# A hybrid decoder trunk on one Trainium2 core: token tiles 2 to 7 of the first layer scaled from a feature-major copy of x in groups of 256 and 512 columns, the residual loaded from that copy

## The chip, the cores and the metric

The kernel runs on one core of a Trainium2 chip. The metric is the device time of one execution in microseconds (us). Five engines work side by side, each through its own instructions in order: PE (matrix products and transposes), DVE (VectorE), ACT (ScalarE), POOL (GpSimd) and SP, which issues most of the DMA transfers. They wait for each other through semaphores.

## The reference

The reference is a two-layer trunk over a residual stream x of 1024 tokens by 1024 features in f32. Each layer is, cut to what matters here:

```python
h = rmsnorm(x, norm1[l])          # x * rsqrt(mean(x*x) + 1e-6) * gain, per token
proj = h @ w_in[l]                # q, k, v of two attentions, and gates
o_a = dilated_mixture(...)        # windowed attention, three dilations
o_b = stick_breaking_attention(...)
merged = g_a * (o_a @ w_br_a) + g_b * (o_b @ w_br_b)
x = x + merged @ w_o[l]
h2 = rmsnorm(x, norm2[l])
x = x + conv_gated_ffn(h2)
```

and a last rmsnorm. What the change touches is the first rmsnorm of the first layer, which turns the input x into h, and the place that the first residual addition reads x from.

## The kernel before, in words

**Layout.** Products contract over features, so h is held feature-major: 128 features on the partitions, eight such blocks (k = 0 to 7), tokens along the free dimension. The 1024 tokens are two halves n = 0, 1 of 512, each of four token tiles of 128. Every f32 operand of a product is held as two fp32r parts, `hh` (rounded by ACT, L146) and `hl` (the rest, by DVE, L154; the helper is `split`), and a product is three matmuls for each k (L188 to L190).

**The start (`first`, from L2021).** It gets h from x tile by tile. SP loads token tile i token-major as `xr` (L2033, 512 KB, four buffers). ACT squares it with a sum over the row (L2063), takes the root (L2066), and DVE the reciprocal (L2067): the token's factor, a column `ss`. Tiles 0 and 1 are scaled token-major on DVE (L2074), turned by PE (`x_t<-xsq`, L2054) and split. For tiles 2 to 7, PE turns the raw tile (`x_t<-xr`, eight transposes of 128x128 for a tile, L2054), ACT copies it out of PSUM (`x_part`, L2083), PE spreads the factor over the partitions by one more transpose (`x_rb`, L2097), DVE multiplies block by block (`h_raw`, L2100, 128x128), and `split` makes `hh` and `hl`. Raw tiles 0 and 1 are turned and copied as well. Each pair of copies is stored to DRAM as `xs` (L2087, 1 MB each, four of them); the residual is loaded from there much later (`x_in`, L471). POOL puts the scaled tiles 0 and 1 together again as `h_raw` (L2120, `again`).

**What reads h first (`head`).** In order: the values of four heads for token tiles 0 to 3 (`v_ps`, 24 matmuls of 128x256 per tile), one pair of key and query products for half 0 (`kq_ps`, then `q_ps`, 24 matmuls of 128x512 each), the values of tiles 4 to 7, the same two products for half 1. `v_ps`, `kq_ps` and `q_ps` take turns in the two PSUM banks of the tag "ps": the values of tiles 4 and 5 use the bank of `kq_ps`, which is free once ACT and DVE have taken `kq_h` and `kq_l` out of it (L605, L606). The weights of the keys and queries (`kq_w`, two chunks each) are loaded by SP (L169, two buffers) and split on POOL (L176, L177). From then on the program is a long run of block products (`i_a`, `i_c` and others) with attention and FFN behind them.

**What sets the order.** PE's order is written out by hand: `mixer` steps the generator `first` and the generator `head` in turn. On ACT, DVE, POOL and SP the order is fixed when the program is built, by priorities; at run time each engine takes its instructions strictly in that order, and an instruction that waits holds all that are behind it.

## Time and profile before

| what | us |
|---|---|
| median of 3 runs | 2603.27 |
| lowest and highest | 2602.32, 2603.33 |
| the profiled execution, its own time | 2603.86 |
| its span, first to last instruction | 2602.2 |
| first `kq_ps` matmul of half 0 starts | 29.19 |
| first `v_ps` matmul of tile 4 starts | 42.23 |
| first `i_a` matmul starts | 65.46 |

The page gives the busy time of each engine, the chain of work that ended last, and the costliest groups of instructions. A row of a group reads: line, engine, operation, output and inputs, shape and count, then busy time, mean ns of one, and the idle time ahead of it with what ended it. A row of the timeline reads: start, length, engine, line, operation, and in brackets the idle time before. Matmuls are pipelined, so a row of eight is shorter than eight times the mean of one. The time of the profiled execution is 1.7 us more than its span.

### The profile page before, as it was taken

How to read it: one execution, taken by the hardware profiler on the slowest of the kernel's cores; microseconds unless marked ns; L12 is line 12 of the kernel's file. 1: busy time of each engine (PE TensorE's matmuls, PEld its weight loads, DVE VectorE, ACT ScalarE, POOL GpSimd, SP SyncE). 2: the span in 40 equal slices, each digit the busy share in tenths (PEclk: the TensorE clock that was granted, in tenths of full speed). 3: DMA queues.
4: the chain of work that ended last, by engine and by line, in shares of the span. 5: the costliest groups of instructions: out<-in, count | busy, mean ns of one | idle time of the engine just before them, and what ended most of it. 6: DMA issues, size and time to landing. Idle time of an engine off the chain costs nothing.

```text
span 2602.2 us, 36060 instructions
## 1 busy us (share of the span) xinstructions
PE 2589.6 (100%) x12647; PEld 2165.4 (83%) x12647; DVE 2084.7 (80%) x3485; ACT 1349.5 (52%) x2521; POOL 105.6 (4%) x145
## 2 busy tenths in 40 slices
PE   9999999999999999999999999999999999999999
PEld 8888888888888888888888888888888888888887
DVE  8877777796888888897677788777869888889965
ACT  6555666664554545422445555666645555554225
POOL 3000000030000000000000000000300000000000
PEclk9999999999999999999999999999999999999999
DMA  7434578863244454688344436798633354447863
GB/s 257 152 119 134 163 207 226 236 235 101 88 148 157 138 176 134 243 325 311 146 147 146 128 127 194 194 235 238 198 99 121 122 171 136 154 162 264 342 242 118
DMA packets 401409, 470.60 MB, mean 181 GB/s; under 512 B 24500, under 2 KB 315980, under 8 KB 399436
## 3 DMA queue, kind: packets, MB, share of 16 engines
q1 hardware_dynamic: 400364, 465.90, 55.2%
q0 software_dynamic: 704, 2.13, 0.4%
q8 instruction: 100, 1.64, 0.3%
q14 instruction: 81, 0.66, 0.1%
q10 hardware_dynamic: 160, 0.27, 0.0%
HBM read 305.59 MB, written 162.63 MB: 180 GB/s over the span
## 4 chain that ended last, share of the span: by engine, by line
PE 93%; DVE 3%; ACT 2%; DMA 1%; issue 1%; SPq 0%; POOL 0%; DVEq 0%; ACTq 0%
PE u_a L1060 6%; PE u_a L1061 6%; PE u_a L1059 6%; PE d_ps L1823 5%; PE d_ps L1825 5%; PE d_ps L1824 5%; PE i_a L1059 5%; PE i_a L1060 5%; PE i_a L1061 5%; PE u_c L1059 3%; PE u_c L1060 3%; PE u_c L1061 3%; PE i_c L1059 2%; PE i_c L1061 2%; PE i_c L1060 2%; PE o_ps L188 2%
## 5 line engine op out<-in xcount | busy, mean ns | idle before, releaser
L146 ACT CAST w_hi<-up_a 128x512 fp32r<-128x512 f32 x280 | 174.0, 622 | 277.1 <-DVE up_a L1677 120.8
L154 DVE TENSOR_TENSOR w_lo<-up_a,w_hi 128x512 fp32r<-128x512 f32 x280 | 189.3, 688 | 83.6 <-ACT w_hi L146 83.6
L146 ACT CAST w_hi<-in_a 128x512 fp32r<-128x512 f32 x252 | 156.2, 622 | 161.8 <-PE i_c L1060 35.6
L154 DVE TENSOR_TENSOR w_lo<-in_a,w_hi 128x512 fp32r<-128x512 f32 x252 | 172.7, 687 | 73.3 <-ACT w_hi L146 64.7
L1834 DVE TENSOR_TENSOR x<-x,d_ps 128x512 f32<-128x512 f32 x220 | 149.9, 683 | 60.3 <-PE d_ps L1825 57.0
L1059 PE MATMUL u_a<-hh,w_hi 128*128 128x512 f32 x320 | 124.5, 389 | 0.0
L1060 PE MATMUL u_a<-hl,w_hi 128*128 128x512 f32 x320 | 124.5, 389 | 0.0
L1061 PE MATMUL u_a<-hh,w_lo 128*128 128x512 f32 x320 | 124.5, 389 | 0.0
L1059 PE MATMUL u_a<-t_hi,w_hi 128*128 128x512 f32 x320 | 124.5, 389 | 0.0
L1060 PE MATMUL u_a<-t_lo,w_hi 128*128 128x512 f32 x320 | 124.5, 389 | 0.0
L1061 PE MATMUL u_a<-t_hi,w_lo 128*128 128x512 f32 x320 | 124.5, 389 | 0.0
L1823 PE MATMUL d_ps<-gd_in,w_hi 128*128 128x512 f32 x316 | 123.2, 390 | 0.0
L1825 PE MATMUL d_ps<-gd_in,w_lo 128*128 128x512 f32 x316 | 123.0, 389 | 0.0
L1824 PE MATMUL d_ps<-gd_in,w_hi 128*128 128x512 f32 x316 | 122.9, 389 | 0.0
L1059 PE MATMUL i_a<-hh,w_hi 128*128 128x512 f32 x288 | 117.9, 410 | 0.0
L1059 PE MATMUL i_a<-t_hi,w_hi 128*128 128x512 f32 x288 | 116.5, 404 | 0.0
L1061 PE MATMUL i_a<-hh,w_lo 128*128 128x512 f32 x288 | 113.1, 393 | 0.0
L1061 PE MATMUL i_a<-t_hi,w_lo 128*128 128x512 f32 x288 | 113.1, 393 | 0.0
L1060 PE MATMUL i_a<-hl,w_hi 128*128 128x512 f32 x288 | 112.9, 392 | 0.0
L1060 PE MATMUL i_a<-t_lo,w_hi 128*128 128x512 f32 x288 | 112.9, 392 | 0.0
L1823 PE MATMUL d_ps<-gd_in,wd 128*128 128x512 f32 x284 | 111.0, 391 | 0.0
L1825 PE MATMUL d_ps<-gd_in,wd 128*128 128x512 f32 x284 | 110.5, 389 | 0.0
(405 smaller groups left out, 7738.7 us busy)
## 6 DMA issues: line engine op xcount, KB each, us to landing
gd<-g SPq DMA_DIRECT2D x154, 512.0 KB, 3.1
gd_in<-gd SPq DMA_DIRECT2D x154, 512.0 KB, 6.2
up_a<-in_w_up_dram SPq DMA_DIRECT2D x80, 512.0 KB, 5.5
in_a<-in_w_in_dram SPq DMA_DIRECT2D x72, 512.0 KB, 5.4
wd_raw<-in_w_down_dram SPq DMA_DIRECT2D x22, 1024.0 KB, 11.4
gin<-gs SPq DMA_DIRECT2D x32, 512.0 KB, 4.3
w_raw<-in_w_o_dram SPq DMA_DIRECT2D x64, 256.0 KB, 2.8
gs<-u SPq DMA_DIRECT2D x48, 256.0 KB, 2.5
```

Of the source, the lines that this page charges most:

```text
L146: one = act.copy(hi, src)
L154: two = dve.tensor_tensor(lo, src, f32(hi), ALU.subtract)
L188: pe.matmul(o, lh, rh, start=(first and i == 0), stop=False, skip_group_check=share)
L1059: pe.matmul(o, w[0][:, c], rh, start=(first and i == 0), stop=False, skip_group_check=True)
L1060: pe.matmul(o, w[0][:, c], rl, start=False, stop=False, skip_group_check=True)
L1061: pe.matmul(o, w[1][:, c], rh, start=False, stop=(last and i == 3), skip_group_check=True)
L1823: pe.matmul(o, wh[:, c], gh, start=(i == 0 and k in (0, 4, 5)), stop=False, skip_group_check=True)
L1824: pe.matmul(o, wh[:, c], gl, start=False, stop=False, skip_group_check=True)
L1825: pe.matmul(o, wl[:, c], gh, start=False, stop=(i == m - 1), skip_group_check=True)
L1834: dve.tensor_tensor(x, x, o, ALU.add)
```

## The change

The program gets a second input, `xt`, which is x turned to feature-major, [128, 8, 1024]; it is laid out with the inputs, ahead of the launch.

Tiles 2 and 3: one load `x_late` of 128x8x256 from `xt`; two factor transposes; eight DVE multiplications of 128x256 instead of sixteen of 128x128; the splits in four pairs of k (128x2x256). Tiles 4 to 7: the half is loaded from `xt` straight into `h_raw` in two transfers of 128x4x512; four factor transposes in one place; eight DVE multiplications of 128x512 in place; eight splits of 128x512. The 64 transposes of raw tiles, the 16 copies out of PSUM and the four stores to `xs` are gone; the token-major tiles `xr` are still loaded, for the squares. The residual of layer 0 is loaded from `xt`.

```diff
-    def x_in(n, h):
+    def x_in(l, n, h):
...
+        src = xs[n][:, 4 * h : 4 * h + 4, :] if l else xt[:, 4 * h : 4 * h + 4, n * HF : (n + 1) * HF]
+        nc.sync.dma_start(X[n][h], src)
...
         def scaled(i):
...
-            ss = factor[i] = sb.tile([P, 8], F32, tag="ss", bufs=2, name="ss")
+            ss = factor[i] = sb.tile([P, 8], F32, tag="ss", bufs=2, name="ss") if i < 4 else wide[:, 2 * (i - 4) :]
             with tc.high_priority(offset=AHEAD):
                 one = act.activation(sq, xr[i], AF.Square, accum_out=ss[:, 0:1])
-                if i >= TWICE + 2:
-                    tc.add_manual_dep(one.ins, LAST["kept" if i == 5 else f"hi{max(2, i - 3)}"], NO_SYNC, reason="behind")
+                if i > 3:
+                    tc.add_manual_dep(one.ins, LAST["hi2"], NO_SYNC, reason="behind")
...
-        def normed(i):
+        def normed(i, many, src):
 
             n, c = i // 4, i % 4
-            if c == 0:
-                new_h(n)
-            if i in (TWICE, 4):
-                raw_h(n)
-            rb = bank("s" if i == TWICE else "o", "x_rb")
-            pe.transpose(rb[:, 0:P], factor[i][:, 2:3].to_broadcast([P, P]), ident)
-            t = slice(c * P, (c + 1) * P)
+            w = many * P
+            rb = bank("s" if n == 0 else "o", "x_rb")
+            for j in range(many):
+                pe.transpose(rb[:, j * P : (j + 1) * P], factor[i + j].to_broadcast([P, P]), ident)
+            t = slice(c * P, c * P + w)
             for k in range(KD):
-                dve.scalar_tensor_tensor(RAW[n, k // 4][:, k % 4, t], part[i][:, k, :], g0[:, k : k + 1], rb[:, 0:P], ALU.mult, ALU.mult)
...
+                h_ = RAW[n, k // 4][:, k % 4, t]
+                dve.scalar_tensor_tensor(h_, src(k), g0[:, k : k + 1], rb[:, 0:w], ALU.mult, ALU.mult)
+                if n or k % 2:
+                    kk = slice(k, k + 1) if n else slice(k - 1, k + 1)
+                    LAST["h"] = split(*(y[:, kk, t] for y in H[n]), RAW[n, k // 4][:, slice(kk.start % 4, kk.start % 4 + kk.stop - kk.start), t]).ins.name
+                    LAST.setdefault(f"hi{i}", LAST["hi"])
...
+        load(3)
+        late = quarter("x_late").rearrange("p a (b c) -> p (a b) c", c=2 * P)
+        nc.sync.dma_start(late, xt[:, :, 2 * P : 4 * P])
+        for i in (4, 5):
+            load(i)
+        raw_h(1)
+        for h in range(2):
+            nc.sync.dma_start(RAW[1, h], xt[:, 4 * h : 4 * h + 4, HF:T])
+        tps[1] = turned(rest[1], "s")
...
+        raw_h(0)
+        with tc.high_priority(offset=AHEAD):
+            normed(2, 2, lambda k: late[:, k, :])
+        yield
+        load(6)
+        load(7)
...
+        new_h(1)
+        normed(4, 4, lambda k: RAW[1, k // 4][:, k % 4, :])
...
+    inputs = {**inputs, "xt": np.asarray(inputs["x"])[0].T.reshape(KD, P, T).transpose(1, 0, 2)}
```

How the order of the instructions moves, at the three places that matter below. A row is a line of the kernel, the operation, what it writes and reads, and the shape; x2 is two alike in a row. Line numbers of the changed kernel are some lines off those of before.

ACT from the square of tile 3 on, before (`hh_194` is the half of tokens 0 to 511):

```order
L2063 ACTIVATE xsq,ss<-xr 128x1024
L2066 ACTIVATE ss<-ss,eps 128x1
L146 CAST hh_194<-h_raw 128x4x128 x2
L2063 ACTIVATE xsq,ss<-xr 128x1024
L585 CAST vb<-v_ps 128x4x2x64
L2066 ACTIVATE ss<-ss,eps 128x1
L2083 COPY x_part<-x_t 128x4x128 x2
L2063 ACTIVATE xsq,ss<-xr 128x1024
L146 CAST hh_194<-h_raw 128x4x128
L2066 ACTIVATE ss<-ss,eps 128x1
L2083 COPY x_part<-x_t 128x4x128 x2
L146 CAST hh_194<-h_raw 128x4x128
```

and in the changed kernel, from the same square on (`hh_195` is the same half; `wide` holds the factors of tiles 4 to 7):

```order
L2065 ACTIVATE xsq,ss<-xr 128x1024
L2068 ACTIVATE ss<-ss,eps 128x1
L146 CAST hh_195<-x_t 128x4x128 x2
L146 CAST hh_195<-h_raw 128x2x256
L2065 ACTIVATE xsq,wide<-xr 128x1024 x2
L146 CAST hh_195<-h_raw 128x2x256
L2068 ACTIVATE wide<-wide,eps 128x1 x2
L2065 ACTIVATE xsq,wide<-xr 128x1024
L146 CAST hh_195<-h_raw 128x2x256
L2068 ACTIVATE wide<-wide,eps 128x1
L2065 ACTIVATE xsq,wide<-xr 128x1024
L146 CAST hh_195<-h_raw 128x2x256
```

Before, both casts of tile 2 stand ahead of the square of tile 4, and the two of tile 3 behind the squares of tiles 4 and 5. Now there are four casts for tiles 2 and 3 together: the first stands ahead of the squares of tiles 4 and 5, the second behind them, the third behind the square of tile 6 and the fourth behind that of tile 7.

SP's transfers from the loads of `xr` 2 and 3 on, before:

```order
L2033 DMA xr<-in_x_dram 128x1024 x2
L169 DMA w_raw<-in_w_in_dram 128x4x128 x2
L2033 DMA xr<-in_x_dram 128x1024 x2
L2087 DMA xs_86<-x_part 1024x1x256
L169 DMA w_raw<-in_w_in_dram 128x4x128 x2
L2033 DMA xr<-in_x_dram 128x1024
```

and now:

```order
L2035 DMA xr<-in_x_dram 128x1024 x2
L2154 DMA x_late<-in_xt_dram 128x8x256
L2035 DMA xr<-in_x_dram 128x1024
L2159 DMA h_raw<-in_xt_dram 128x4x512
L2035 DMA xr<-in_x_dram 128x1024
L2159 DMA h_raw<-in_xt_dram 128x4x512
L2035 DMA xr<-in_x_dram 128x1024 x2
L169 DMA w_raw<-in_w_in_dram 128x4x128 x2
```

The three transfers from `xt` stand between the tiles, and the key weights (L169) have gone from behind tile 3 to behind tile 7.

DVE around `kq_l`, which frees the PSUM bank that the values of tile 4 need, before (`hl_444` is the half of tokens 512 to 1023):

```order
L2100 SCALAR_TENSOR_TENSOR h_raw<-x_part,g_85,x_rb 128x128 x6
L154 TENSOR_TENSOR hl_444<-h_raw,hh_443 128x4x128
L606 TENSOR_TENSOR kq_l<-kq_ps,kq_h 128x512
L154 TENSOR_TENSOR hl_444<-h_raw,hh_443 128x4x128
L2100 SCALAR_TENSOR_TENSOR h_raw<-x_part,g_85,x_rb 128x128 x8
```

and now (`hl_438` is the same half):

```order
L2091 SCALAR_TENSOR_TENSOR h_raw<-h_raw,g_85,x_rb 128x512 x3
L154 TENSOR_TENSOR hl_438<-h_raw,hh_437 128x512 x3
L2091 SCALAR_TENSOR_TENSOR h_raw<-h_raw,g_85,x_rb 128x512 x3
L154 TENSOR_TENSOR hl_438<-h_raw,hh_437 128x512 x3
L2091 SCALAR_TENSOR_TENSOR h_raw<-h_raw,g_85,x_rb 128x512 x2
L607 TENSOR_TENSOR kq_l<-kq_ps,kq_h 128x512
L154 TENSOR_TENSOR hl_438<-h_raw,hh_437 128x512 x2
```

`kq_l` now stands behind eight multiplications and six splits of the whole second half. On PE the 64 transposes of raw tiles are gone from between the products and the four factor transposes of tiles 4 to 7 stand together in the middle of `kq_ps`; nothing else moves there, and on no engine does the order differ after the first layer's early block products, but for the source of the residual's four loads.

More of the change, by code (lines that the diff above doesn't have):

```diff
@@ L65, in trunk_kernel @@
 @with_exitstack
-def trunk_kernel(ctx, tc, x, norm1, w_in, b_gate, w_br, w_o, norm2, w_up, conv_w, conv_b, w_down, norm_f, out, depth=None, probe=None):
+def trunk_kernel(ctx, tc, x, xt, norm1, w_in, b_gate, w_br, w_o, norm2, w_up, conv_w, conv_b, w_down, norm_f, out, depth=None, probe=None):
     nc = tc.nc
@@ L470, in x_in @@
         X[n][h] = quarter(f"x{n}")
-        nc.sync.dma_start(X[n][h], xs[n][:, 4 * h : 4 * h + 4, :])
+        src = xs[n][:, 4 * h : 4 * h + 4, :] if l else xt[:, 4 * h : 4 * h + 4, n * HF : (n + 1) * HF]
+        nc.sync.dma_start(X[n][h], src)
     ACC = [None, None]
@@ L1467, in mixer @@
                     late_x = X_AT.index(i)
-                    x_in(late_x // 2, late_x % 2)
+                    x_in(l, late_x // 2, late_x % 2)
             gt = gts[i]
@@ L2025, in first @@
         act.activation(warm[:, 0:1], eps, AF.Sqrt)
-        xr, rest, tps, parts, factor, raw_t, part = {}, {}, {}, {}, {}, {}, {}
+        xr, rest, tps, parts, factor = {}, {}, {}, {}, {}
+        wide = cp.tile([P, 16], F32, name="wide")
         raw = big("w_raw").rearrange("p a (b c) -> p (a b) c", c=256)
@@ L2060, in scaled @@
             sq = rest[i] = rest["pair"][:, i % 2, :] if i < 4 else sb.tile([P, T], F32, tag="ot", name="xsq")
-            ss = factor[i] = sb.tile([P, 8], F32, tag="ss", bufs=2, name="ss")
+            ss = factor[i] = sb.tile([P, 8], F32, tag="ss", bufs=2, name="ss") if i < 4 else wide[:, 2 * (i - 4) :]
             with tc.high_priority(offset=AHEAD):
                 one = act.activation(sq, xr[i], AF.Square, accum_out=ss[:, 0:1])
-                if i >= TWICE + 2:
-                    tc.add_manual_dep(one.ins, LAST["kept" if i == 5 else f"hi{max(2, i - 3)}"], NO_SYNC, reason="behind")
+                if i > 3:
+                    tc.add_manual_dep(one.ins, LAST["hi2"], NO_SYNC, reason="behind")
                 act.activation(ss[:, 1:2], ss[:, 0:1], AF.Sqrt, bias=eps[:, 0:1], scale=1.0 / D)
-                one = dve.reciprocal(ss[:, 2:3], ss[:, 1:2])
+                to = ss[:, 2:3] if i < 4 else wide[:, 8 + i - 4 : 9 + i - 4]
+                one = dve.reciprocal(to, ss[:, 1:2])
+                factor[i] = to
             if i == 0:
@@ L2073, in scaled @@
                     hd = slice(h * HF, (h + 1) * HF)
-                    dve.scalar_tensor_tensor(sq[:, hd], xr[i][:, hd], ss[:, 2:3], gb[h], ALU.mult, ALU.mult)
+                    dve.scalar_tensor_tensor(sq[:, hd], xr[i][:, hd], to, gb[h], ALU.mult, ALU.mult)
             yield
-        def kept(i):
-            if i % 2 == 0:
-                both = part["pair"] = quarter("x_part", F32, 2 * P).rearrange("p k (i t) -> p k i t", i=2)
-                part[i], part[i + 1] = both[:, :, 0, :], both[:, :, 1, :]
-            for h in range(2):
-                one = act.copy(part[i][:, 4 * h : 4 * h + 4, :], raw_t[i][h])
-            if i == 3:
-                LAST["kept"] = one.ins.name
-            if i % 2:
-                nc.sync.dma_start(xs[i // 4][:, :, (i % 4 - 1) * P : (i % 4 + 1) * P], part["pair"].rearrange("p k i t -> p k (i t)"))
@@ L2089, in normed @@
-        def normed(i):
-            n, c = i // 4, i % 4
-            if c == 0:
-                new_h(n)
-            if i in (TWICE, 4):
-                raw_h(n)
-            rb = bank("s" if i == TWICE else "o", "x_rb")
-            pe.transpose(rb[:, 0:P], factor[i][:, 2:3].to_broadcast([P, P]), ident)
-            t = slice(c * P, (c + 1) * P)
-            for k in range(KD):
-                dve.scalar_tensor_tensor(RAW[n, k // 4][:, k % 4, t], part[i][:, k, :], g0[:, k : k + 1], rb[:, 0:P], ALU.mult, ALU.mult)
-            if i < 7:
-                for _ in f[i + 1]:
-                    pass
-            for h in range(2):
-                LAST["h"] = split(*(y[:, 4 * h : 4 * h + 4, t] for y in H[n]), RAW[n, h][:, :, t]).ins.name
-            LAST[f"hi{i}"] = LAST["hi"]
+        def normed(i, many, src):
+            n, c = i // 4, i % 4
+            w = many * P
[3 more added lines that the diff above has]
+            t = slice(c * P, c * P + w)
+            for k in range(KD):
+                h_ = RAW[n, k // 4][:, k % 4, t]
[4 more added lines that the diff above has]
+                    LAST.setdefault(f"hi{i}", LAST["hi"])
@@ L2162, in first @@
         yield
-        for i in range(1, 8):
-            load(i + 2)
-            if i >= TWICE:
-                if i == TWICE:
-                    raw_t[i - 1] = turned(xr[i - 1], "t")
-                    kept(i - 1)
-                raw_t[i] = turned(xr[i], "o" if i == TWICE else "st"[i % 2])
-                with tc.high_priority(offset=AHEAD) if i == TWICE else nullcontext():
-                    kept(i)
-                    normed(i)
-                if i in (4, 5):
-                    again(i - 4)
-            else:
-                raw_t[i - 1] = turned(xr[i - 1], "t")
-                tps[i] = turned(rest[i], "s")
-                if i < 7:
-                    for _ in f[i + 1]:
-                        pass
-                in_two(i)
-                kept(i - 1)
-            yield
+        load(3)
[7 more added lines that the diff above has]
+        tps[1] = turned(rest[1], "s")
+        for i in (2, 3):
+            for _ in f[i]:
+                pass
+        in_two(1)
+        yield
+        raw_h(0)
+        with tc.high_priority(offset=AHEAD):
+            normed(2, 2, lambda k: late[:, k, :])
+        yield
+        load(6)
+        load(7)
+        yield
+        for i in (4, 5):
+            for _ in f[i]:
+                pass
+        again(0)
+        yield
+        for i in (6, 7):
+            for _ in f[i]:
+                pass
+        again(1)
+        yield
+        new_h(1)
+        normed(4, 4, lambda k: RAW[1, k // 4][:, k % 4, :])
+        yield
     def setup(l):
@@ L2207, in trunk_kernel @@
             pending = ffn(l, pending, enter(l + 1) if l + 1 < depth else leave)
-_INS = ["x", "norm1", "w_in", "b_gate", "w_br", "w_o", "norm2", "w_up", "conv_w", "conv_b", "w_down", "norm_f"]
+_INS = ["x", "xt", "norm1", "w_in", "b_gate", "w_br", "w_o", "norm2", "w_up", "conv_w", "conv_b", "w_down", "norm_f"]
 def kernel(**inputs):
```

## The prediction, made blind

> **What bounds the kernel now.** I read the engines' busy times first, then the chain of work that ended last.

> ```profile
> PE 2589.6 (100%) x12647; PEld 2165.4 (83%) x12647; DVE 2084.7 (80%) x3485; ACT 1349.5 (52%) x2521; POOL 105.6 (4%) x145
> PE 93%; DVE 3%; ACT 2%; DMA 1%; issue 1%; SPq 0%; POOL 0%; DVEq 0%; ACTq 0%
> ```

> PE is busy for 2589.6 of 2602.2 us. So a matmul taken away shortens the run if its results were not all that PE was kept waiting by, and each us for which PE waits lengthens it. All that changes lies in the first 50 us; the timeline of PE there:

> ```profile
> 16.50 0.36 PE L188 MATMUL v_ps<-w_hi,hh 128*128 128x256 f32 x1
> 19.33 0.28 PE L190 MATMUL v_ps<-w_hi,hl 128*128 128x256 f32 x1
> 19.45 1.04 PE L2054 MATMUL x_t<-ident,xr 128*128 128x128 f32 x8
> 20.32 0.27 PE L2097 MATMUL x_rb<-ident,ss 128*128 128x128 f32 x1
> 29.19 0.48 PE L188 MATMUL kq_ps<-hh,kq_w 128*128 128x512 f32 x1
> 36.69 0.48 PE L188 MATMUL q_ps<-hh,kq_w 128*128 128x512 f32 x1
> 42.23 0.28 PE L188 MATMUL v_ps<-w_hi,hh 128*128 128x256 f32 x1
> L2054 PE MATMUL x_t<-ident,xr 128*128 128x128 f32 x64 | 8.2, 274 | 0.3 <-ACT x_part L2083 0.3
> PE warm L2127 <- POOL ident masks.py:199: 1.8, 1, 1.8
> ```

> The 24 value matmuls of a tile go from 16.50 to 19.45, 0.12 us apart; eight transposes take 0.87 (19.45 to 20.32); 24 products of 512 columns 5.54 (36.69 to 42.23). PE's longest wait is the 1.8 us at the very start. Two marks serve below: kq_ps at 29.19, values of tile 4 at 42.23, 13.04 apart, two tiles' transposes between them included.

> **What is removed.** 64 transposes, 8 x 0.87 = 7.0 us of PE. That is the most that can be won, 0.27%. The 16 copies on ACT and the stores of xs are gone too; neither engine bounds the run.

> **When the data come now.** The transfers of one queue land in the order of issue; the rows that show it and their pace:

> ```profile
> 11.64 1.06 ACT L2063 ACTIVATE xsq<-xr 128x1024 f32<-128x1024 f32 x1 [0.32 <-DMA xr<-in_x_dram]
> 13.83 0.61 POOL L176 CAST kq_w<-w_raw 128x512 fp32r<-128x512 f32 x1 [0.42 <-DMA w_raw<-in_w_in_dram]
> 14.67 0.61 POOL L176 CAST kq_w<-w_raw 128x512 fp32r<-128x512 f32 x1 [0.23 <-DMA w_raw<-in_w_in_dram]
> xr<-in_x_dram SPq DMA_DIRECT2D x8, 512.0 KB, 4.4
> 8.00:14.00 6.00, 5.78 (x44) 4.95 (x43) 4.17 (x9) 5.61 (x13) 2.70 (x3) 1.00 1.07 374
> 8.80:11.40 2.60, 2.38 (x19) 2.11 (x19) 2.48 (x6) 2.49 (x6) 0.52 (x1) 1.00 1.03 409
> ```

> ACT waits for tile 2 until 11.64, and 0.79 MB (tile 3 and a chunk of key weights) and 1.05 MB later POOL is let go at 13.83 and 14.67: 346 GB/s to the second. The last columns of the windows are the DMA share and GB/s: 374 with the engines full, 409 in the best stretch, so I take 374, with 346 and 409 as ends. Tile 3 keeps its place. Behind it now come x_late (1.05 MB), tile 4 (0.52), half of the second half (1.05), tile 5, the other half, tiles 6 and 7, and only then the key weights. Counted from 11.64 in MB behind tile 2: x_late 1.57, tile 5 3.67, tile 6 5.24, tile 7 5.77, key weights 6.03 and 6.29. At 374: 15.8, 21.5, 25.7, 27.1, 27.8 and 28.5 us. Issue keeps ahead: each tile's buffer is freed by work that ends by 15 us.

> **What the first half waits for.** ACT's order puts the casts of tiles 2 and 3 between the squares. What the operations take:

> ```profile
> L2063 ACT ACTIVATE xsq<-xr 128x1024 f32<-128x1024 f32 x8 | 8.5, 1065 | 2.1 <-DMA xr<-in_x_dram 2.1
> L2063 ACT ACTIVATION_READ_ACCUMULATOR xsq<-xr 128x1 f32 x8 | 1.5, 193 | 0.0
> L2066 ACT ACTIVATE ss<-ss,eps 128x1 f32<-128x1 f32 x8 | 2.4, 295 | 0.2
> L146 ACT CAST hh<-h_raw 128x512 fp32r<-128x512 f32 x16 | 9.8, 623 | 3.3 <-DVE h_raw L2100 3.3
> 38.38 2.15 DVE L2100 SCALAR_TENSOR_TENSOR h_raw<-x_part,g,x_rb 128x128 f32<-128x128 f32 x8
> 13.62 1.29 DVE L154 TENSOR_TENSOR hl<-x_t,hh 128x512 fp32r<-128x512 f32 x2 [0.31 <-ACT hh L146]
> 10.52 1.40 DVE L2074 SCALAR_TENSOR_TENSOR xsq<-xr,ss,gb 128x512 f32<-128x512 f32 x2
> ```

> A DVE multiplication costs 0.27 at 128 columns (2.15/8) and 0.70 at 512 (1.40/2); at 256, which no row shows, I take 0.41 on the line between, its bounds 0.27 and 0.70. It hardly matters, since ACT is late. DVE's splits of tile 1 (to 14.9 before) now stand behind the square of tile 3, some 1.5 later; two multiplications follow, and the first cast goes at about 17.4. Then the square of tile 5 stands waiting for its tile until 21.5 and the second cast, ready to go at 19.6, comes at 22.7. The square of tile 6 starts at 25.7 and ends with its sum read at 26.8; third cast 27.5; root 27.7; square of tile 7 to 28.8, read 29.0, root 29.3; fourth cast 29.9; split on DVE 30.6. PE is fed in four sips, then has half a us of tile 2 and the 24 matmuls of tile 3 (2.9) left: kq_ps starts at 34.0 instead of 29.19, **4.8 later**, all 48 transposes ahead of it already gone. With 409 GB/s 3.6 (ACT, not the transfers, then sets the pace), with 346 5.9.

> **What the second half waits for.** kq_ps's 24 matmuls have the four factor transposes in their middle: 2.8 + 0.4 after their start, DVE can begin.

> ```profile
> L154 DVE TENSOR_TENSOR hl<-h_raw,hh x6: 684/1098/1242, 19.3 to 30.1; 128x512 fp32r<-128x512 f32 x6
> L154 DVE TENSOR_TENSOR hl<-h_raw,hh x6: 675/688/693, 33.2 to 41.2; 128x512 fp32r<-128x512 f32 x6
> 37.15 0.68 DVE L606 TENSOR_TENSOR kq_l<-kq_ps,kq_h 128x512 fp32r<-128x512 f32 x1
> 17.73 3.29 POOL L2120 TENSOR_TENSOR h_raw<-hh,hl 128x256 f32<-128x256 f32 x4
> 28.73 3.73 POOL L2120 TENSOR_TENSOR h_raw<-hh,hl 128x256 f32<-128x256 f32 x4
> L177 POOL TENSOR_TENSOR kq_w<-w_raw,kq_w x4: 1273/1293/1798, 15.2 to 27.5; 128x512 fp32r<-128x512 f32 x4
> ```

> The bank for the values of tile 4 comes free with kq_l, before at 37.8, far ahead of need; now behind eight multiplications (5.6) and six splits. A split takes about 0.60 in a row where POOL is idle (0.69 alone) and 1.1 while POOL computes, as it does from 19 to 30 us now and would until about 43. I take half of the six at 1.0: 4.8 (bounds 3.6 and 6.6). With 0.7 for kq_l and 0.1 of hand-over: 3.2 + 5.6 + 4.8 + 0.8 = 14.4 from kq_ps to the values of tile 4, against 13.04 before: **1.4 more** (0.2 to 3.2). The weights do not add to it: key weights land at 27.8, cast 0.6 and rest 1.3 on POOL, ready 29.7 for use at 34.0; query weights, behind the second chunk and four sums (31.6 + 3.7), are ready at 37.2 to 38.2 for use at 40. Without that cover, each us of lateness would be one of PE.

> **What follows.** From tile 4 on the orders are as before. DVE's next sums start 1.2 behind that mark, before 0.4 ahead of its like, so DVE is 1.6 later against PE.

> ```profile
> 41.83 1.28 DVE L1082 TENSOR_TENSOR h_sum<-h_raw 128x512 f32<-128x512 f32 x2
> 48.80 0.69 DVE L586 TENSOR_TENSOR vb<-v_ps,vb 128x512 fp32r<-128x512 f32 x1 [1.06 <-ACT vb L585]
> 60.03 0.69 DVE L606 TENSOR_TENSOR kq_l<-kq_ps,kq_h 128x512 fp32r<-128x512 f32 x1 [1.17 <-ACT kq_h L605]
> L471 SPq DMA_DIRECT2D x<-xs x4: 319/406/457, 512.2 to 538.8; - x4
> L1328 DVE TENSOR_TENSOR x<-x,o_ps x16: 673/686/689, 586.9 to 665.6; 128x512 f32<-128x512 f32 x16
> DMA to landing us min/median/max: 6.1/6.1/6.1
> ```

> Its two waits on PE's results, 2.2 us, take that up. The residual's loads keep their size and land in 6.1 us, 48 us ahead of their first use: nothing, even at several times the length.

> **The sum.** 4.8 + 1.4 = +6.2, the 7.0 us of removed PE work already inside. The profiled execution's span goes from 2602.2 to 2608.4, its own time from 2603.86 to 2610.1; it stands 0.6 above the median, so the median goes from 2603.27 to about 2609.5. Ends: 3.6 + 0.2 = 3.8 and 5.9 + 3.2 = 9.1, so 2607.1 to 2612.4.

> [...]

> **The rivals.**

> *PE loses its pace in the gaps.* Between the sips PE would stand still from about 19.3 to 23.4, then 2.9 and 1.3 us. At its first start in this trace, out of idleness, PE was slow:

> ```profile
> 1.81 1.65 PE L2127 MATMUL warm<-ident 128*128 128x128 f32 x6 [1.81 <-POOL ident masks.py:199]
> 3.92 1.97 PE L2143 MATMUL gb<-ident,g 128*128 128x128 f32 x8 [0.26 <-DVE g L2140]
> L2143 PE MATMUL gb<-ident,g x8: 417/417/472, 3.9 to 5.5; 128*128 128x128 f32 x8
> ```

> Eight of 128x128 took 1.97 us there, 417 ns for one, against 1.04 and 274 later: half the pace from 1.81 to about 5.9, that is 2 us lost. If a gap brings that back, the matmuls of tile 3 and the first of kq_ps pay it: +8.2, 2611.5. Against it: no gap of before is long enough to show it after the start. The granted clock reads 1.00 throughout, the slow start included, so it will not tell.
> [...]

> *Fast transfers, quiet DVE.* The transfers keep 409 and the splits run free of POOL: +3.8 to +5, about 2607.5.

> *Not slower.* The squares do not hold the casts, because tiles 4 to 7 land well before the sums above. Then the pairs go at DVE's and ACT's own pace, 0.8 + 0.6 + 0.7 each from 16.4, the last at 24.9; tile 3 ends and kq_ps starts at 28.3, 0.9 early, and with the quick second half (0.2) the time is 2602.6. It decides where tile 7 lands before some 24 us. Against it: that takes 470 GB/s, which no window shows.

> *The whole 7.0 won*, 2596.3, needs kq_ps at 24 us, when tile 3 is not yet scaled: no chance worth a number.

> **How the numbers follow.** Forecast 0.5, slow PE 0.25, fast transfers 0.15, not slower 0.1. A measurement of this kernel tells about 0.2%, 5.2 us, from no change: the line is 2608.5. Above it lie nearly nine tenths of the forecast's share, all of the slow PE's and a fifth of the fast transfers': 0.72. Faster by over 0.2% gets 0.04 of the last case, no change the rest, 0.24. The range, 2605.5 to 2613.5, takes in the forecast's ends and the slow PE.

> **What would show it.** Right: on ACT, the second cast of tiles 2 and 3 behind the square of tile 5 at about 22, waiting for DMA; kq_ps at 33 to 36; the values of tile 4 starting with kq_l's end, a wait of PE of 2 to 3 us. Slow PE: tile 3's value matmuls 0.24 apart. Wrong: PE without waits over 1 us between 19 and 30, or kq_ps held by POOL.

## The result and the profile after

The changed kernel takes 2609.96 us (median of 8 runs, 2608.61 to 2610.93) against 2602.29 (8 runs, 2601.91 to 2603.51) of the kernel before beside it: ratio 1.0026, 95% interval 1.0017 to 1.0035. It is slower by 7.7 us. The profiled execution's span is 2608.6 us, 6.4 above that of before. The page's first part:

```profile
PE 2587.5 (99%) x12583; PEld 2162.3 (83%) x12583; DVE 2082.0 (80%) x3453; ACT 1341.6 (51%) x2505; POOL 104.9 (4%) x145
```

PE has 64 instructions fewer and is busy 2.1 us less, not 7.0, and the run is longer all the same: PE waits more, and part of its work is slower. The view of waits gives for each waiting line the us in total, the times, and the longest:

```profile
PE v_ps L188 <- ACT hh L146: 5.6, 3, 3.2
PE v_ps L188 <- DVE kq_l L607: 2.4, 1, 2.4
PE warm L2116 <- POOL ident masks.py:199: 1.8, 1, 1.8
```

The first two rows are new. They are the casts of tiles 2 and 3 and the PSUM bank of the values of tile 4. The timeline of ACT (start, length, and the idle time ahead with what ended it) shows where the first comes from:

```profile
17.03 0.62 ACT L146 CAST hh<-h_raw 128x512 fp32r<-128x512 f32 x1 [1.67 <-DVE h_raw L2091]
21.21 1.06 ACT L2065 ACTIVATE xsq<-xr 128x1024 f32<-128x1024 f32 x1 [2.51 <-DMA xr<-in_x_dram]
22.27 0.60 ACT L146 CAST hh<-h_raw 128x512 fp32r<-128x512 f32 x1
25.28 1.06 ACT L2065 ACTIVATE xsq<-xr 128x1024 f32<-128x1024 f32 x1 [2.03 <-DMA xr<-in_x_dram]
26.33 0.60 ACT L146 CAST hh<-h_raw 128x512 fp32r<-128x512 f32 x1
27.04 1.04 ACT L2065 ACTIVATE xsq<-xr 128x1024 f32<-128x1024 f32 x1
28.48 0.62 ACT L146 CAST hh<-h_raw 128x512 fp32r<-128x512 f32 x1
```

The second cast stands behind a square that waits 2.51 us for tile 5, the third behind one that waits 2.03 for tile 6, the fourth behind that of tile 7. The timeline of PE, at the last of the four sips, at the end of a slow stretch in tile 3, and at the two marks:

```profile
29.15 0.58 PE L188 MATMUL v_ps<-w_hi,hh 128*128 128x256 f32 x1 [0.21 <-ACT hh L146]
32.38 0.41 PE L188 MATMUL v_ps<-w_hi,hh 128*128 128x256 f32 x1
32.60 0.40 PE L189 MATMUL v_ps<-w_lo,hh 128*128 128x256 f32 x1
33.07 0.28 PE L189 MATMUL v_ps<-w_lo,hh 128*128 128x256 f32 x1
33.19 0.28 PE L190 MATMUL v_ps<-w_hi,hl 128*128 128x256 f32 x1
34.74 0.40 PE L188 MATMUL kq_ps<-hh,kq_w 128*128 128x512 f32 x1
48.70 0.36 PE L188 MATMUL v_ps<-w_hi,hh 128*128 128x256 f32 x1 [2.42 <-DVE kq_l L607]
```

kq_ps starts at 34.74 (before 29.19), the values of tile 4 at 48.70 (before 42.23). Up to 32.8 the value matmuls are 0.22 us apart, behind it 0.12. The windows of the same kernel give the reason in the column behind POOL, the granted TensorE clock (the last two are DMA share and GB/s):

```profile
10.00:20.00 10.00, 7.79 (x60) 6.85 (x58) 6.05 (x13) 6.94 (x16) 2.53 (x2) 1.00 1.05 388
20.00:30.00 10.00, 4.70 (x14) 3.37 (x14) 4.20 (x12) 6.31 (x14) 2.58 (x3) 0.63 0.66 232
30.00:40.00 10.00, 9.92 (x54) 9.00 (x55) 3.20 (x6) 1.65 (x3) 9.76 (x13) 0.86 0.47 140
40.00:50.00 10.00, 7.58 (x39) 6.21 (x38) 10.00 (x16) 5.92 (x10) 2.65 (x3) 1.00 0.76 221
50.00:60.00 10.00, 10.00 (x74) 10.00 (x73) 8.77 (x15) 3.56 (x8) 0.00 (x0) 0.83 0.33 106
```

The clock falls twice: 0.63 between 20 and 30 (still 0.86 in the next ten), and 0.83 between 50 and 60. Last, the timeline of DVE: two multiplications of the first half, and the second half up to `kq_l`:

```profile
16.13 0.87 DVE L2091 SCALAR_TENSOR_TENSOR h_raw<-x_late,g,x_rb 128x256 f32<-128x256 f32 x2
40.10 2.75 DVE L154 TENSOR_TENSOR hl<-h_raw,hh 128x512 fp32r<-128x512 f32 x3
44.75 1.88 DVE L154 TENSOR_TENSOR hl<-h_raw,hh 128x512 fp32r<-128x512 f32 x3
47.87 0.68 DVE L607 TENSOR_TENSOR kq_l<-kq_ps,kq_h 128x512 fp32r<-128x512 f32 x1
```

The two multiplications of 256 columns take 0.87, 0.43 each. kq_l goes at 47.87, behind six splits that take 4.63 together, and PE follows at 48.70.

### The profile page after: what moved, and what is told of

It reads as the page before. It is cut to its first block, busy times and chain, and to the rows that moved or that the text cites. A ratio compares the mean times of both kernels' runs of the same rounds, so it can differ in the third digit from the quotient of the medians.

```text
span 2608.6 us, 35868 instructions
## 1 busy us (share of the span) xinstructions
PE 2587.5 (99%) x12583; PEld 2162.3 (83%) x12583; DVE 2082.0 (80%) x3453; ACT 1341.6 (51%) x2505; POOL 104.9 (4%) x145
## 4 chain that ended last, share of the span: by engine, by line
PE 95%; DVE 2%; ACT 1%; DMA 1%; issue 0%; SPq 0%; DVEq 0%; ACTq 0%
PE u_a L1060 6%; PE u_a L1062 6%; PE u_a L1061 6%; PE d_ps L1824 5%; PE d_ps L1825 5%; PE d_ps L1826 5%; PE i_a L1060 5%; PE i_a L1061 5%; PE i_a L1062 5%; PE u_c L1060 3%; PE u_c L1062 3%; PE u_c L1061 3%; PE i_c L1060 2%; PE i_c L1062 2%; PE i_c L1061 2%; PE o_ps L188 2%
## 5 line engine op out<-in xcount | busy, mean ns | idle before, releaser
L146 ACT CAST w_hi<-up_a 128x512 fp32r<-128x512 f32 x280 | 174.0, 622 | 277.3 <-DVE up_a L1678 120.5
L154 DVE TENSOR_TENSOR w_lo<-up_a,w_hi 128x512 fp32r<-128x512 f32 x280 | 189.5, 689 | 83.3 <-ACT w_hi L146 83.3
L146 ACT CAST w_hi<-in_a 128x512 fp32r<-128x512 f32 x252 | 156.2, 622 | 160.6 <-PE i_c L1061 35.9
L154 DVE TENSOR_TENSOR w_lo<-in_a,w_hi 128x512 fp32r<-128x512 f32 x252 | 172.8, 688 | 73.6 <-ACT w_hi L146 66.4
## 6 DMA issues: line engine op xcount, KB each, us to landing
gd<-g SPq DMA_DIRECT2D x154, 512.0 KB, 2.7
gd_in<-gd SPq DMA_DIRECT2D x154, 512.0 KB, 6.4
up_a<-in_w_up_dram SPq DMA_DIRECT2D x80, 512.0 KB, 5.2
in_a<-in_w_in_dram SPq DMA_DIRECT2D x72, 512.0 KB, 5.2
gin<-gs SPq DMA_DIRECT2D x32, 512.0 KB, 4.1
```

The lines of the kernel that those rows point to most:

```text
L146: one = act.copy(hi, src)
L154: two = dve.tensor_tensor(lo, src, f32(hi), ALU.subtract)
```

## The experiments

Single executions differ far behind the change: a wait of PE of 1.1 us on ACT's `p1h` (L663, second layer) stands in the profile of before and not in those of the changed kernel or of e5_resid, so spans say less than early marks. From kq_ps of half 1 to the first score matmul (`z`, near 80 us) every kernel takes 22.67 or 22.68 us, so the early stretches carry the comparison. All times are us; x_rb is the first factor transpose of tiles 2 and 3, ahead of which the changed kernels only differ in their start (15.2 to 16.8). In the first column, kernels that share the order of all engines up to kq_ps differ by 0.3 to 1.0 from one profiled execution to another (e1_casts and e6_casts_kql, changed and e4_kql, e7b_early_rb and e8_q_early), so smaller differences there tell nothing.

| kernel | x_rb to kq_ps | kq_ps to values of tile 4 | values of tile 4 to kq_ps of half 1 | z starts | median of runs | ratio to before (95%) |
|---|---|---|---|---|---|---|
| before | – | 13.04 | 11.51 | 76.41 | 2602.3 to 2602.9 | 1 |
| changed | 19.08 | 13.96 | 13.08 | 84.45 | 2609.96 | 1.0026 (1.0017–1.0035) |
| e1_casts | 14.06 | 16.24 | 14.19 | 82.64 | 2608.01 | 1.0019 (1.0010–1.0028) |
| e2_tiles | 17.81 | 14.27 | 13.06 | 83.55 | 2610.29 | 1.0030 (1.0018–1.0041) |
| e3_fill | 17.67 | 15.31 | 11.59 | 83.45 | 2611.12 | 1.0033 (1.0020–1.0045) |
| e4_kql | 19.56 | 11.38 | 13.21 | 82.07 | 2608.51 | 1.0024 (1.0014–1.0034) |
| e5_resid | – | – | – | 76.4 | 2602.13 | 0.9999 (0.9990–1.0008) |
| e6_casts_kql | 13.75 | 12.57 | 15.35 | 79.79 | 2605.00 | 1.0009 (1.0000–1.0018) |
| e7a_early | 11.35 | 11.37 | 13.20 | 74.25 | 2600.06 | 0.9990 (0.9981–0.9999) |
| e7b_early_rb | 12.73 | 10.97 | 12.93 | 75.23 | 2600.51 | 0.9993 (0.9984–1.0002) |
| e8_q_early | 11.76 | 10.98 | 11.52 | 72.17 | 2598.74 | 0.9985 (0.9976–0.9994) |
| e9_no_lag | 16.27 | 11.38 | 13.22 | 79.50 | 2604.11 | 1.0006 (0.9997–1.0015) |
| e3b_fill_half | 20.10 | 13.30 | 11.59 | 83.29 | 2612.40 | 1.0034 (1.0022–1.0047) |
| e3c_fill_fit | 17.58 | 14.36 | 11.59 | 82.95 | 2609.20 | 1.0024 (1.0015–1.0033) |

### The order of the casts: e1_casts

```diff
-                    LAST.setdefault(f"hi{i}", LAST["hi"])
+                    LAST[f"hi{i}"] = LAST["hi"]
```

The squares of tiles 4 to 7 now stand behind all four casts.

> The changed kernel with one line altered: the squares of tiles 4 to 7 are put behind the last of the four casts of tiles 2 and 3 on ACT, not behind the first. Theory (the casts were held by squares that waited for their tiles): the four casts follow each other about 2.2 us apart, the last by 24.5 instead of 29.1; the value matmuls of tile 3 end near 28.4; kq_ps then waits for the first chunk of key weights until about 29.5, so it starts near 29 instead of 34.7; the values of tile 4 start near 43.3 instead of 48.7. Time about 2604.6, 5.4 less than the changed kernel. Rival (what holds PE is the length of the work on 256 columns or the loads from xt as such): the last cast stays near 29 and the time within 1 us of 2610.

The casts go 2.2 apart, at DVE's and ACT's own pace; the timeline of ACT has the last at

```profile
23.34 0.62 ACT L146 CAST hh<-h_raw 128x512 fp32r<-128x512 f32 x1 [1.54 <-DVE h_raw L2091]
```

instead of 28.48, and kq_ps comes 5.2 earlier, at 29.54. So the squares did hold the casts. But 2.3 are given back in the next stretch and 1.1 in the one behind it: the time is 2608.01, 2.0 below the changed kernel, where 5.4 were forecast. The waits, then DVE's timeline of this run:

```profile
PE v_ps L188 <- DVE kq_l L607: 3.6, 1, 3.6
```

```profile
34.91 3.41 DVE L154 TENSOR_TENSOR hl<-h_raw,hh 128x512 fp32r<-128x512 f32 x3
40.22 3.49 DVE L154 TENSOR_TENSOR hl<-h_raw,hh 128x512 fp32r<-128x512 f32 x3
```

POOL's work did not move (27.8 to 43.2), so all six splits ahead of kq_l now lie beside it and take 1.15 each (6.90, against 4.63). That is the 2.3, and the bank's wait grows to 3.6. (Inside the same stretch PE also waits 0.7 in q_ps for the query weights from POOL.) The clock falls again behind the bank's wait, to 0.50 from 44.9 to 51.7.

### The order of the loads: e2_tiles

```diff
-        raw_h(1)
-        for h in range(2):
-            nc.sync.dma_start(RAW[1, h], xt[:, 4 * h : 4 * h + 4, HF:T])
...
         load(6)
         load(7)
+        raw_h(1)
+        for h in range(2):
+            nc.sync.dma_start(RAW[1, h], xt[:, 4 * h : 4 * h + 4, HF:T])
```

> The changed kernel with only the order of the loads altered: tiles 4 to 7 are loaded ahead of the two halves of h_raw, so that tile 5 lands near 18.3, tile 6 near 19.7 and tile 7 near 21.0 instead of 21.2, 25.3 and 27. ACT's order stays nearly as it is. Theory (landing of the tiles together with the order on ACT): the casts are let go, the last near 26, tile 3 ends near 30.2 and kq_ps starts there; time about 2605.6, a little more than with the squares moved. Rival (the order on ACT alone costs it, whatever the landing): the last cast stays near 29 and the time near 2610.

Only one of the two transfers moved: SP's order is fixed by priorities, and the first still stood ahead of tile 5. Tile 5, whose place had not changed, came 0.5 earlier and tile 6 at least 2.4; the third and the fourth cast came 1.1 earlier, kq_ps 1.2 (33.54). The time, 2610.29, did not fall; 2605.6 was forecast for the full order. The casts agree with the theory that they follow the squares, but this is no test of the full order; e7a_early has that, together with other edits.

### The pace of PE: e3_fill, e3b_fill_half, e3c_fill_fit

```diff
+GAPS = {2: {2: 24, 4: 14}, 4: {0: 18}}
...
         for i, ((lh, ll), (rh, rl)) in enumerate(pairs):
+            if i in gaps:
+                early["fill"](gaps[i])
```

Idle matmuls stand in PE's gaps: so many of them ahead of so many pairs of a tile. In e3b_fill_half the line reads `{2: {2: 12, 4: 8}, 4: {0: 9}}`, in e3c_fill_fit `{2: {2: 12, 4: 14, 6: 4}, 4: {0: 9}}`.

> The changed kernel with idle transposes of 128x128 into an unused bank on PE: 24 ahead of the second pair of k of tile 2, 14 ahead of the third, 18 ahead of the values of tile 4. They fit into the waits (2.6 of 3.25 us, 1.5 of 2.1, 2.0 of 2.4). Theory (PE's clock falls in the gaps and comes back only after some us of work): the granted clock stays 1.00 from 20 to 60 us, the value matmuls of tile 3 and of tile 4 stand 0.12 us apart throughout, kq_ps starts 1.3 earlier, near 33.4, and 1.5 more is won at tile 4: time about 2607.2. Rival (those matmuls are slow for what they read): the spacing of 0.21 stays and the time is 2610 or more.

The clock was 1.00 in every window and all value matmuls 0.12 apart, but each idle matmul stands in the trace as two (24 as 48, 14 as 28), and the fillings of 5.5 and 3.3 us outlasted the gaps: kq_ps gained only 0.9. The time was 2611.12, a miss against the 2607.2 that was forecast.

> The changed kernel with idle matmuls in PE's three gaps again, now half as many (12 and 8 in tile 2, 9 ahead of tile 4), so that they end inside the gaps. If the pace that PE lost is the clock's alone: granted clock 1.00 in every window from 10 to 80, value matmuls 0.12 apart, kq_ps at 33.4 (34.74 less 1.3), values of tile 4 at 47.4 behind kq_l as before, kq_ps of half 1 at 58.9 instead of 61.78: 2607.2, 2.8 below the changed kernel. If the slow pace comes from the operands (they arrive late, or DVE and POOL disturb), it stays and so does the time.

A miss in the first half: 1.6 us of the second gap stayed empty, the clock was 0.51 between 28 and 32 all the same, and kq_ps came at 35.73. The second half did as expected, 11.59 instead of 13.08. The time was 2612.40, the highest of all and a second miss (2607.2 was forecast): both this run and e3_fill show a wait of PE of 1.6 to 1.8 on ACT's `u` (`u_c`, in the FFN) that no other kernel has. Why is open; e3c_fill_fit, which differs from them in the counts alone, has it not.

> The changed kernel with idle matmuls fitted to the gaps the half-filled run still left (12, 14 and 4 in tile 2, 9 ahead of tile 4; there 1.6 of the second gap stayed empty and the clock fell for 7 us all the same). If PE's lost pace is the clock's and the clock goes by how much PE had to do in the last few us: granted clock 1.00 in every window from 10 to 60, value matmuls of tile 3 0.12 apart, kq_ps at 33.0 to 33.6 (34.74 in the changed kernel), kq_ps of half 1 24.9 later, at 58 to 58.6 (61.78): 3.2 to 3.8 earlier than the changed kernel, 2606.5; with the late wait of 1.7 on ACT's u that both filled runs had, 2608. If the clock falls again in tile 3, kq_ps stays at 34.5 or later and fullness is not what it goes by.

Windows of e3c_fill_fit:

```profile
20.00:30.00 10.00, 9.30 (x80) 8.90 (x78) 3.67 (x12) 5.95 (x14) 1.79 (x2) 1.00 0.72 253
30.00:40.00 10.00, 9.56 (x59) 8.39 (x58) 4.39 (x7) 2.39 (x5) 9.76 (x13) 1.00 0.51 147
50.00:60.00 10.00, 10.00 (x86) 10.00 (x85) 9.80 (x17) 4.00 (x8) 0.00 (x0) 1.00 0.33 105
```

No loss of clock, 1.5 less to kq_ps (17.58) and 1.5 less in the values of tiles 4 to 7 (11.59). kq_ps stood at 34.33, not 33.0 to 33.6, because this execution began 1.1 later (x_rb at 16.75 against 15.66); the time, 2609.20, fell by less than 1 us against the changed kernel, where 2.6 to z were won from x_rb and 2606.5 was forecast. So the clock costs about 3 us of the changed kernel's early stretches. The 1.5 of the second half is alike in three runs. The 1.5 of the first half is less sure: counted from the end of the last cast to kq_ps it is 1.2 (5.64 in the changed kernel, 4.45 here). Filling the gaps wins little of this in time.

### The bank: e4_kql

```diff
-        LAST["head"] = [x.name for x in in_parts(c, SCALE, hi, lo, o)]
+        with tc.high_priority(offset=AHEAD) if soon else nullcontext():
+            LAST["head"] = [x.name for x in in_parts(c, SCALE, hi, lo, o)]
...
-            yield from kq_half(0, wk, n)
+            yield from kq_half(0, wk, n, not l and n == 0)
```

> The changed kernel with kq_l of half 0 given priority, so that it stands on DVE behind the first three multiplications and splits and not behind all eight multiplications. Theory (the values of tile 4 wait for the bank that kq_l frees): they start near 46, right behind q_ps, then wait in the middle for the last two splits near 49.7; the bank's share is about 1.5 us, and up to 1.5 more if the clock holds without the 2.4 us gap: time 2607 to 2608.5. Rival (the wait was for the splits anyway): within 0.5 us of 2610.

The values of tile 4 start right behind q_ps (46.19, 11.38 behind kq_ps instead of 13.96). A shorter wait stands inside tile 4 instead (0.9, for the last casts and splits), the clock stays at 1.00 there, and z starts 2.4 earlier. The time is 2608.51, at the upper end of the forecast.

### The residual: e5_resid

The kernel before, with the new source in `x_in` alone.

> The kernel before, with one thing changed: the residual of layer 0 is loaded from xt instead of xs (the copies and the stores to xs stay). By the prediction this costs nothing, the loads land 48 us ahead of their first use: 2602.3, within 0.7 of before, and all waits of the first 60 us as before. If the other layout of the source cost something that the early waits hide in the sum, it would show here as 1 us or more.

2602.13 against 2602.70, ratio 0.9999: the new source costs nothing that can be told.

### Both edits, and the loads early: e6_casts_kql, e7a_early, e9_no_lag

e6_casts_kql is e1_casts and e4_kql together.

> The changed kernel with both one-line edits: squares of tiles 4 to 7 behind all four casts of tiles 2 and 3, and kq_h, kq_l of half 0 ahead of the second half's splits. If the two waits are separate and add: kq_ps at 29.5, values of tile 4 right behind q_ps at 41.5 to 42.5, then waits inside tile 4 until DVE's last split at about 48.5 (POOL still beside it), kq_ps of half 1 at 57.5 to 59.5 against 61.8: about 2606, 4 below the changed kernel. If what is won early is only handed on to DVE (it bounds the second half whatever the bank does), kq_ps of half 1 stays at 60 or later and the time at 2608, as with the first edit alone.

2605.00; kq_ps of half 1 at 57.12. The two waits are separate and their removal adds: z starts 1.8 earlier with the first edit, 2.4 with the second, 4.7 with both. The clock still falls twice, behind tile 2, where PE never stood still for more than 0.7 us at once, and behind tile 4, where its gaps were 0.9 and 0.7 (below).

e7a_early is e6_casts_kql with

```diff
-                if n or k % 2:
-                    kk = slice(k, k + 1) if n else slice(k - 1, k + 1)
+                kks = [slice(k, k + 1)] if n else {3: [slice(0, 2)], 5: [slice(2, 4)], 7: [slice(4, 6), slice(6, 8)]}.get(k, [])
+                for kk in kks:
...
+            one = nc.sync.dma_start(RAW[1, h], xt[:, 4 * h : 4 * h + 4, HF:T])
+            tc.add_manual_dep(one.ins, LAST["raw"][1], NO_SYNC, reason="behind")
+            tc.add_manual_dep(one.ins, LAST["xr"], NO_SYNC, reason="behind")
```

where `LAST["raw"][1]` is the load of the second chunk of key weights and `LAST["xr"]` that of tile 7.

> The two edits of the run before, and: the splits of tiles 2 and 3 one pair of blocks behind the multiplications on DVE, and on SP the key weights behind tile 4, tiles 5 to 7 next, the two halves of the second half's h_raw last. If the first half is bound by transfers and by DVE's chain of multiplication, cast, split: fourth split at 22.2, kq_ps at 26 to 27.5, PE without a gap over 1 us there and a granted clock of 1.0 until 30. Key weights are ready on POOL at 21, so POOL's share of the second half ends about 37. Second half bound by DVE: from x_rb at about 30, 5.5 of multiplications, 7 to 8 of splits, 1.4 of kq_l: last split at 44 to 45, kq_ps of half 1 at 53.5 to 55 (before: 53.74): 2602 to 2604. If PE loses its clock in tile 3 all the same, 1.3 later.

2600.06, better than forecast and below the kernel before: kq_ps at 27.00, kq_ps of half 1 at 51.57, the clock at 1.00 in every window from 10 to 60. e9_no_lag takes the order of DVE's splits back and keeps the loads.

> The kernel with all loads early (2600.06), but with the splits of tiles 2 and 3 right behind their multiplications again, as in the change. Tells what the two orders are worth: if the order of DVE gave the first half's 2.2, kq_ps goes back to 29.2, PE's gaps of 0.7 come back with a granted clock near 0.6 in 24 to 28, and with POOL early the second half keeps 24.6 from kq_ps to kq_ps of half 1: 53.8, 2602.3. If the early key weights gave it all: kq_ps stays at 27 and the time at 2600.

kq_ps went back by more than expected, to 32.23. With the key weights early, POOL now works beside the splits of tiles 2 and 3. The four of them in e9_no_lag (shortest, median, longest ns):

```profile
L154 DVE TENSOR_TENSOR hl<-h_raw,hh x4: 797/914/1048, 18.0 to 25.0; 128x512 fp32r<-128x512 f32 x4
```

and in e6_casts_kql, where the key weights land later:

```profile
L154 DVE TENSOR_TENSOR hl<-h_raw,hh x4: 691/692/693, 17.5 to 24.0; 128x512 fp32r<-128x512 f32 x4
```

In the order multiplication, cast, split each slower split delays the next pair, and the gaps add up until the clock falls (0.67 in 24 to 28, 0.50 in 28 to 32). With the splits one pair behind, the multiplications run on while ACT casts. So the early key weights, and the other loads in their new order, help the second half (24.6 from kq_ps to kq_ps of half 1, against 27.9 in e6_casts_kql) and hurt the first, unless DVE's order is changed too.

### The factors early: e7b_early_rb, e8_q_early

e7b_early_rb takes a `yield` away, which puts the factor transposes of tiles 4 to 7 ahead of kq_ps; e8_q_early also has `kq_half(1, wq, n, not l and n == 0)`.

> The run before, with the factor transposes of tiles 4 to 7 ahead of kq_ps instead of in its middle. If DVE bounds the second half, everything there comes 2 to 2.8 earlier: last split at 41.5 to 43, kq_ps of half 1 at 51 to 53: 2599.5 to 2602, at or below the kernel before. If the factors are the limit instead (tile 7 lands at 22.4, its factor is ready about 26.5), PE waits up to 1 us at x_rb and the gain is under 1.

> The run with the early factor transposes, and kq_l of q_ps (half 0) ahead of the block sums on DVE too. There the values of tile 6 waited 1.16 for it. If that wait is all that the early transposes gave back: kq_ps at 28.7, no wait of PE over 0.3 from there to 75, kq_ps of half 1 at 51.4 (before: 53.74): 2599.3. If DVE is full (the splits of the second half come late instead), a wait of about 1 comes back inside tiles 4 to 6 and the time stays at 2600.5.

e7b_early_rb gave 2600.51, no better than e7a_early: DVE was ready earlier, but the values of tile 6 waited 1.16 for kq_l of q_ps, which stood behind the block sums. e8_q_early moves that too: no wait of PE is shown from 27 to 72, 11.52 for the values of tiles 4 to 7 (the same as before), 2598.74 us, 3.9 below the kernel before and 11.2 below the changed one. (That kq_ps came 1.7 earlier than in e7b_early_rb is not this edit's doing; up to there the order of every engine is the same. Its own part is the 1.4 between 12.93 and 11.52.) Its windows:

```profile
20.00:30.00 10.00, 8.57 (x57) 7.59 (x57) 7.06 (x14) 7.96 (x17) 8.62 (x10) 1.00 0.93 318
30.00:40.00 10.00, 10.00 (x53) 8.60 (x53) 10.00 (x16) 5.51 (x9) 5.86 (x6) 1.00 0.94 280
40.00:50.00 10.00, 10.00 (x84) 9.91 (x83) 10.00 (x17) 4.10 (x8) 0.00 (x0) 1.00 0.38 125
```

PE is full from 30 on, and DVE has nothing left: it too is busy throughout 30 to 50.

## Why the prediction came out right, and where it did not

The predicted time, 2609.5, is 0.5 below the median. The sum behind it was +6.2, where z came 8.0 later and the median rose by 7.7: the mechanisms held, a term was missing, and the time fits as well as it does by luck: the 2603.27 from which it was counted lies 1.0 above the median of before beside the result.

**The removed work** is gone as reckoned: 64 transposes fewer. That these 7.0 are a bound stands; e8_q_early wins 3.9 of them.

**When the data come.** Tile 5 landed at 21.21 (predicted 21.5), tile 6 at 25.28 (25.7); 388 GB/s from 10 to 20, between the 374 taken and the end of 409. The last three casts ended at 22.87, 26.93 and 29.10, where the working had 22.7, 27.5 and 29.9.

**The first half** was forecast 4.8 later, kq_ps at 34.0; it was 5.55 later, at 34.74. e1_casts shows that the squares were the cause (5.0 of x_rb to kq_ps go with that one line). Two errors lie in the term, and they nearly cancel: the last cast came 0.8 earlier than reckoned, which leaves 4.0, and the clock adds the 1.2 to 1.5 that e3c_fill_fit does without. Together 5.2 to 5.5. The 0.41 taken for a multiplication of 256 columns was 0.43.

**The second half** was forecast 14.4 from kq_ps to the values of tile 4; 13.96 was measured, with the six splits at 4.63 for the 4.8 taken. e4_kql confirms the bank. The weights cost nothing, as reckoned: no wait of PE for POOL is shown there. That the orders cost nothing from tile 4 on was wrong by 1.6: 13.08 instead of 11.51, and e3_fill, e3b_fill_half and e3c_fill_fit give it to the clock, 11.59 each.

**The rival of the slow PE**, 0.25, is what failed to get its due: it occurred, and twice. Its size in the first half, 2.0, was near the 1.5 measured. Its second place was not seen, because the argument priced only the gaps between the sips, the longest 4.1 us; the clock fell again behind a wait of 2.42, to 0.50 from 49.92 to 53.34. And the sentence that the granted clock will not tell was wrong: it reads 0.63 from 20 to 30, and 0.50 in all of 22.61 to 32.85. The 1.00 at the slow start misled: in the trace of before the record of the clock begins only at 6.71 us, and a window without a record reads 1.00. As a difference to before, its +8.2 was nearer to the measured 7.7 than the forecast's +6.2.

**Fast transfers, quiet DVE** had neither condition met: 388 GB/s in place of 409, and six splits of 4.63 in place of 3.6. **Not slower** had the mechanism that e1_casts then made by order instead of by faster transfers: kq_ps at 29.54.

**The residual** at nothing: e5_resid shows it. (The 48 us of the prediction count from the issue of the last load, at 538.8, to the first use at 586.9; behind its landing 42 are left.)

## What to carry to other kernels

Before taking work off the engine that bounds, follow what the new loads do to the order of the engines that feed it: here one square per tile, waiting for its transfer ahead of a cast that was ready, held the first half up by 5.0, and a late `kq_l` and the lost clock came on top. Price a gap of PE twice, once for the wait and once for what may run behind it at half clock (0.50 for 3.4 to 10.2 us in the runs here), and do so for a row of short gaps too (0.70 at most in tile 2 of e6_casts_kql). Let a tile that frees a bank, or a multiplication that the next cast waits for, go ahead of work that only has to be done some time.

## What the runs showed of the hardware

**The clock fell without one long gap, and in these runs for 3.4, 6.8 or 10.2 us.** In e6_casts_kql the longest gap in tile 2 is 0.70; its windows (PE's busy time is the first behind the length):

```profile
22.00:23.00 1.00, 0.78 (x5) 0.57 (x6) 1.00 (x3) 0.00 (x0) 0.00 (x0) 1.00 1.06 414
23.00:24.00 1.00, 0.30 (x4) 0.10 (x2) 0.32 (x2) 0.69 (x2) 0.00 (x0) 0.85 1.02 408
26.00:27.00 1.00, 1.00 (x6) 1.00 (x6) 0.43 (x3) 1.00 (x5) 0.00 (x0) 0.50 0.42 109
27.00:28.00 1.00, 1.00 (x9) 1.00 (x9) 0.07 (x1) 0.97 (x3) 0.34 (x1) 0.95 0.06 18
```

In windows of 0.25 us the clock reads 0.50 from 23.75 to 27.00, 0.88 and 0.79 in the one ahead and the one behind, and 1.00 around them: the slow stretch goes from 23.69 to 27.11, 3.4 us. Its second one goes from 47.6 to 51.0. In the changed kernel the same windows give 22.61 to 32.85:

```profile
22.00:23.00 1.00, 0.08 (x1) 0.08 (x1) 0.10 (x1) 1.00 (x5) 0.00 (x0) 0.81 1.05 412
32.00:33.00 1.00, 1.00 (x7) 1.00 (x7) 0.00 (x0) 0.00 (x0) 1.00 (x2) 0.57 0.02 6
```

```profile
19.20:22.61 3.41, 0.47 (x4) 0.27 (x3) 0.00 (x0) 1.40 (x3) 0.00 (x0) 1.00 1.05 394
22.61:26.03 3.42, 1.95 (x6) 1.43 (x6) 1.61 (x5) 1.39 (x4) 0.00 (x0) 0.50 1.04 348
26.03:29.44 3.41, 2.24 (x7) 1.73 (x8) 2.03 (x6) 3.38 (x9) 2.02 (x3) 0.50 0.10 28
29.44:32.85 3.41, 3.27 (x15) 2.98 (x15) 1.19 (x2) 0.14 (x1) 3.33 (x5) 0.50 0.29 79
```

```profile
18.10:21.51 3.41, 1.66 (x14) 1.45 (x13) 1.14 (x3) 1.48 (x3) 0.00 (x0) 1.00 1.04 407
21.51:24.92 3.41, 1.24 (x6) 0.83 (x6) 1.61 (x5) 3.14 (x8) 0.00 (x0) 1.00 1.03 385
```

In the changed kernel PE was busy for 0.47 of the 3.41 us ahead of the fall. The clock stayed at 0.50 behind steps of 1.95 and 2.24 and was 1.00 again behind one of 3.27: by this count the sips of tile 2 kept it down. In all runs it came back behind steps with PE busy for 0.91 of the time or more, and stayed at 0.50 behind those of 0.84 or less. The steps ahead of the eleven falls have 0.13 to 0.58. But a low share alone did not bring a fall: in e2_tiles 1.66 of 3.41 left the clock at 1.00. e8_q_early and e7b_early_rb had gaps of 0.7 to 1.2 in the same place, a busy share of 0.64 and 0.52 from 20 to 24, and kept 1.00. What decides on a fall no run settles.

**In a row, each further split on DVE took 0.60 while POOL was idle (two in 1.28 at 48.47 in the changed kernel); beside POOL's work one took up to 1.77 (e8_q_early).** The multiplications, which read one operand from PSUM, stayed at 0.69 a piece beside it (e1_casts, three in 2.07). Two places of e8_q_early, each with what POOL does meanwhile:

```profile
21.29 1.77 DVE L154 TENSOR_TENSOR hl<-h_raw,hh 128x512 fp32r<-128x512 f32 x1
19.10 3.42 POOL L179 TENSOR_TENSOR kq_w<-w_raw,kq_w 128x512 fp32r<-128x512 f32 x2
34.78 1.28 DVE L154 TENSOR_TENSOR hl<-h_raw,hh 128x512 fp32r<-128x512 f32 x2
34.96 0.95 POOL L688 MEMSET slots<- 64x1024 f32 x1
```

Beside the MEMSET, which reads no tile, the two splits go as fast as beside an idle POOL. Which of POOL's work slows a split, and why, no run settles.
